# First two units of a stage alternate slab by slab, the norm's squares are added on VectorE, the first x pieces come by ScalarE's queue

## The chip, the cores and the metric

The kernel runs on one core of one Trainium2 chip. A core has TensorE (PE, matrix products into PSUM), VectorE (DVE), ScalarE (ACT), GpSimd (POOL) and SyncE (SP), each with its own in-order stream of instructions, and DMA queues that they start. The metric is the time of one execution in device microseconds (us); lower is better. Times are medians of several runs; the profile is of one further execution.

## The reference, cut to what matters

Two layers over 256 tokens of width 1024, then one last RMSNorm:

```python
for l in range(2):
    h = h + 0.5 * swiglu(rms_norm(h, ffn1_norm[l]), ...)       # 1024 -> 2816 -> 1024
    h = h + hybrid_mixer(rms_norm(h, mix_norm[l]), ...)        # z = u @ w_in, four head groups, @ w_out
    h = h + cross_attention(rms_norm(h, xattn_norm[l]), rms_norm(mem, mem_norm[l]), ...)
    h = h + 0.5 * swiglu(rms_norm(h, ffn2_norm[l]), ...)
return rms_norm(h, final_norm)

def rms_norm(x, g): return x * rsqrt(mean(x * x) + eps) * g
```

All is float32. Each stage starts with a norm of h and then a projection of all of h, so its first product needs every column of h that the stage before has just written.

## The kernel before, in words

**Layout.** `h` holds the stream transposed: 8 blocks k of 128 channels by 256 tokens. `xs` holds h times the norm's gain, each block split into a high part (ACT, L295) and the rest (DVE, L296) in the format fp32r; a product is three part products, made as one matmul of 512 columns (L361, high weights on both parts of x) and one of 256 (L362, low weights on the high part). Such a couple is called a pair below. The factor 1/rms is not in `xs`: it is applied to the products behind, so the products can start before the norm is known.

**Weights.** They come from one array in slabs of 128 by 1024 (512 KB), in the order in which `slab_plan` lists them, by SP's queue (L203) into 4 raw buffers, and each is split into high (ACT, L218) and low (DVE, L219) into 5 buffers `whl`. `W.get` hands out the next slab, splits up to 4 ahead and loads further ahead.

**Units.** A unit is 256 output columns: two slabs (i = 0 with k 0 to 3, i = 1 with k 4 to 7) of 8 pairs each, summed in one of two PSUM buffers `pj`. `proj_T` (and `pair_of` in the feed-forward stages) does a unit: slab 0, slab 1, then `join` copies the result out (ACT L369, DVE L370), which frees the PSUM buffer. After each slab `flush` runs one entry of the list `later`; that is how the norm's end is placed: `norm.rstd()` after the third slab of a stage, its use (`row_bcast`, L342) after the fourth.

**Stage starts.** `ffn` begins with units gate 0 and up 0, the mixer with qa and ka, cross attention with wq 0 and wq 1 (behind the unit V3 of the memory's projections), then `scores(0)`, which needs q of head 0. The stage before ends with `new_rows` for four pieces j of h (blocks 2j and 2j+1): split into `xs`, then `norm.add`: ACT squares the piece (L318) and POOL adds it to `acc` (L319). `rstd` adds the two halves of `acc` (POOL, L324), sums over channels on PE (L330) and takes the power on POOL (L335).

**Start of the kernel.** SP issues, in turn, a piece of x (L274), the channel constants `ch` (L276) and the slabs. **What sets the order.** The kernel is written for a framework whose planner sets each engine's order ahead of time, from its own estimates: it may put an instruction ahead of one that was written earlier if it expects that one to be held up. On the chip the order so made is fixed; an engine waits at an instruction whose inputs are late.

Of the kernel before, what the change touches and what calls it, by code (L numbers as in the profile page):

```python
# [49 lines left out]
def slab_plan():  # L50

    plan = []
    for l in range(L):
        for f in ("ffn1", "ffn2"):
            if f == "ffn2":
                plan += [("z:" + u, l, i, 1040 if "+" in u else 1024) for u in Z_ORDER for i in range(2)]
                plan += [("kv:" + u, l, i, 1024) for u in KV_EARLY for i in range(2)]
                plan += [("w_out", l, k, 1024) for k in range(KD)]
                plan += [("kv:" + u, l, i, 1024) for u in KV_LATE for i in range(2)]
                plan += [("wq:%d" % hd, l, i, 1024) for hd in range(4) for i in range(2)]  # L60
                plan += [("wo", l, k, 1024) for k in range(KD)]
            plan += [(f + ":%s:%d" % (a, g), l, i, 1024) for g in range(NG) for a in "gu" for i in range(2)]
            plan += [(f + ":dn", l, i, 1024) for i in range(NG * 2)]
    return plan

# [175 lines left out]
def trunk(ctx: ExitStack, tc: tile.TileContext, xT, memT, wall, chan, gateb, dlam, t5, poolw, c128, small, out):  # L241
# [29 lines left out]
    h = res.tile([128, KD, T], F32, name="h")  # L271
    ch = const.tile([128, N_CHAN], F32, name="ch")
    for j in range(4):
        nc.sync.dma_start(out=h[:, 2 * j:2 * j + 2, :], in_=xT[:, 512 * j:512 * j + 512].rearrange("p (a b) -> p a b", a=2))  # L274
        if j == 0:
            nc.sync.dma_start(out=ch[:], in_=chan)  # L276
        W.load()
    cc = const.tile([128, 1024], F32, name="cc")
    ident = cc[:, 0:128]
# [18 lines left out]
    class Norm:  # L298
# [12 lines left out]
        def add(self, src):  # L311
            if self.acc is None:
                self.acc = ztile("acc")[:, 0:512]
                S.activation(out=pair(self.acc), in_=src, func=AF.Square)
                self.rows = [self.acc[:, 0:256], self.acc[:, 256:512]]
                return
            sq = ztile("sq")[:, 0:512]
            S.activation(out=pair(sq), in_=src, func=AF.Square)  # L318
            G.tensor_tensor(out=self.acc, in0=self.acc, in1=sq, op=ALU.add)  # L319

        def rstd(self):
            rows = self.rows
# [12 lines left out]
            self.last = G.tensor_tensor(out=r[:], in0=m[:], in1=nhalf[:, 0:2], op=ALU.pow)  # L335
            return r
# [59 lines left out]

    def proj_T(units, l, x, evac):

        for u in units:
            p = pproj()  # L400
            for i in range(2):
                w = W.get(u, l, i, 256)
                for kk in range(4):
                    k = 4 * i + kk
                    for n in range(2):
                        mm2(p[:, n * 512:n * 512 + 512], parts(w, kk, slice(n * 128, n * 128 + 128)), x(k), k == 0, k == KD - 1)
                flush()
            evac(u, join(p))

    def proj_M(u, l, x, width):  # L410

# [52 lines left out]

    def ffn(l, name, norm, c_next, extra=()):
        fs, rbs = [], []
        def pair_of(u):

            p = pproj()
            for i in range(2):  # L470
                w = W.get(u, l, i, 256)
                for kk in range(4):
                    k = 4 * i + kk
                    for n in range(2):
                        mm2(p[:, n * 512:n * 512 + 512], parts(w, kk, slice(n * 128, n * 128 + 128)), xk(k), k == 0, k == KD - 1)
                flush()
            return join(p)

        for g in range(NG):
            gate = pair_of(name + ":g:%d" % g)  # L480

            def act(g=g, gate=gate):
                if g == 0:
                    rbs[0] = row_bcast(rbs[0])
                V.tensor_tensor(out=pair(gate[:, 0:512]), in0=pair(gate[:, 0:512]), in1=twice(rbs[0]), op=ALU.mult)  # L485
                S.activation(out=gate[:, 0:512], in_=gate[:, 0:512], func=AF.Silu)  # L486
                if g == 0:
                    rb05 = sm.tile([128, T], F32, name="rb05", tag="rb05", bufs=1)
                    S.activation(out=rb05[:], in_=rbs[0][:], func=AF.Copy, scale=0.5)
                    rbs.append(rb05)  # L490

            if g == 0:
                later.append(lambda: rbs.append(norm.rstd()))
                later.append(act)
            else:
                act()
            up = pair_of(name + ":u:%d" % g)
# [5 lines left out]
            fs.append(f)  # L503
            for e in dict(extra).get(g, ()):
                e()
        nxt = Norm(quick=c_next is None)
# [181 lines left out]
    def mixer(l, norm, c_next):  # L688
# [42 lines left out]

        def emit(u):

            if u in ("qa", "ka", "pb"):
                w = 15 if u == "pb" else 3
                t = ztile(u)
                tv = t[:, 0:2 * (T + w)].rearrange("p (a b) -> p a b", a=2)
                G.memset(tv[:, :, 0:w], 0.0)

                def ev(_, p):  # L740
                    def go():
                        V.tensor_tensor(out=tv[:, :, w:w + T], in0=pair(p[:, 0:512]), in1=twice(rstd()[1]), op=ALU.mult)
                    if u == "qa":
                        later.append(lambda: R.append(norm.rstd()))
                        later.append(go)
                    else:
                        go()
                proj_T(["z:" + u], l, xk, ev)
                z[u] = tv
# [363 lines left out]
    def cross(l, norm, kv, c_next):  # L1113
# [5 lines left out]

        def wq(hd):  # L1120

            q = big.tile([128, 1024], F32R, name="xq", tag="m", bufs=4)
            proj_T(["wq:%d" % hd], l, xk, lambda _, p: halves(p, q))
            st["q", hd] = q
            if hd == 0:
                def scale():
                    r = norm.rstd()
                    r16 = sm.tile([128, 2], F32, name="r16", tag="r16")
                    V.tensor_scalar(out=r16[:], in0=r[:], scalar1=1.0 / 16, scalar2=None, op0=ALU.mult)
                    R.append(r16)  # L1130
                later.append(scale)

        def scores(hd):
            qt, kt = st["q", hd], kv["K%d" % hd]
# [37 lines left out]
            halves(p, os_[hd])  # L1172

        wq(0)
        wq(1)
        scores(0)
        wq(2)
        scores(1)
# [43 lines left out]
```

## Time and profile before

| | us |
|---|---|
| median of 3 runs | 1213.91 (1213.82 to 1214.43) |
| the profiled execution, its own time | 1216.12 |
| its span from first to last instruction | 1214.3 |
| PE busy | 1192.7 |
| DVE busy | 864.0 |
| ACT busy | 691.2 |
| POOL busy | 109.6 |

The profile gives for each engine the instructions in order of time, what ended the idle time before one, and, for stretches, the clock that was granted to PE (1.00 is its full 2.4 GHz, 0.50 is 1.2 GHz). "issue" means that nothing in the profile explains the time.

### The profile page before, as it was taken

The numbers are of one execution on the slowest core, as the hardware profiler recorded it, in microseconds if no ns is written. First come the engines' busy times: TensorE is split into PE (matmuls) and PEld (weight loads), VectorE is DVE, ScalarE is ACT, GpSimd is POOL, SyncE is SP. The second block draws the span as 40 slices with busy tenths as digits, with TensorE's granted clock in tenths as the row PEclk, the third lists the DMA queues.
The fourth block names the chain that finished last, engine by engine and source line by source line (L and its number), as shares of the span: only waits on it lengthen the run. The fifth ranks groups of instructions, "written<-read, shape, count | busy, mean of one in ns | idle before, by whom it ended". The sixth has DMA issues, their size and how long they took to land.

```text
span 1214.3 us, 18603 instructions
## 1 busy us (share of the span) xinstructions
PE 1192.7 (98%) x7199; PEld 1050.2 (86%) x7199; DVE 864.0 (71%) x1214; ACT 691.2 (57%) x1038; POOL 109.6 (9%) x107
## 2 busy tenths in 40 slices
PE   8999999999999999999999999999999999999996
PEld 6788888988899988888888888898889998888886
DVE  5887667869667677775677776786785867777653
ACT  6766555556556555554555555555664655655552
POOL 4130001104010100000010000011220202000000
PEclk9999999999999999999999999999999999999998
DMA  8866765554445355656556567645535534555650
GB/s 267 281 203 193 225 194 174 162 185 151 144 140 191 105 188 183 197 181 199 189 172 196 184 194 225 190 161 170 183 128 163 172 131 139 185 194 183 197 178 35
DMA packets 63032, 216.48 MB, mean 178 GB/s; under 512 B 7712, under 2 KB 8112, under 8 KB 62944
## 3 DMA queue, kind: packets, MB, share of 16 engines
q1 hardware_dynamic: 61632, 212.11, 54.6%
q0 software_dynamic: 1024, 2.80, 0.8%
q8 instruction: 56, 0.92, 0.3%
q10 hardware_dynamic: 288, 0.39, 0.1%
q14 instruction: 32, 0.26, 0.1%
HBM read 210.01 MB, written 2.11 MB: 175 GB/s over the span
## 4 chain that ended last, share of the span: by engine, by line
PE 89%; DVE 6%; issue 2%; ACT 1%; DMA 1%; POOL 0%; SPq 0%; POOLq 0%; DVEq 0%; ACTq 0%
PE pj L361 49%; PE pj L362 25%; PE pj L355 2%; PE pj L356 2%; DVE whl L219 2%; PE pj L357 2%; PE pj L423 2%; DVE xs L296 1%; ACT whl L218 1%; DMA selt<-in_c_dram 1%; PE pq L357 0%; PE pq L356 0%; PE pq L355 0%; PE pq L956 0%; DMA raw<-in_wall_dram 0%
## 5 line engine op out<-in xcount | busy, mean ns | idle before, releaser
L361 PE MATMUL pj<-xs,whl 128*128 128x512 f32 x1760 | 620.9, 396 | 8.6 <-DVE xs L296 6.4
L219 DVE TENSOR_TENSOR whl<-raw,whl 128x1024 fp32r<-128x1024 f32 (+1 forms) x391 | 483.4, 1239 | 165.6 <-ACT whl L218 160.8
L218 ACT CAST whl<-raw 128x1024 fp32r<-128x1024 f32 (+1 forms) x391 | 406.0, 1042 | 177.1 <-PE pj L362 98.3
L362 PE MATMUL pj<-xs,whl 128*128 128x256 f32 x1760 | 494.6, 281 | 0.1
L361 PEld LDWEIGHTS pj<-xs,whl 128*128 128x128 f32 x1760 | 332.7, 189 | 84.6 <-DVE xs L296 9.1
L362 PEld LDWEIGHTS pj<-xs,whl 128*128 128x128 f32 x1760 | 334.9, 190 | 1.8 <-issue 0.9
L361 PE MATMUL pj<-fs,whl 128*128 128x512 f32 x704 | 244.6, 392 | 0.1
L369 ACT COPY jn<-pj 128x512 f32<-128x512 f32 x147 | 85.6, 582 | 226.6 <-PE pj L362 222.7
L370 DVE TENSOR_TENSOR jn<-pj,jn 128x512 f32<-128x512 f32 x147 | 100.9, 686 | 137.9 <-ACT jn L369 137.8
L362 PE MATMUL pj<-fs,whl 128*128 128x256 f32 x704 | 197.0, 280 | 0.0
L361 PEld LDWEIGHTS pj<-fs,whl 128*128 128x128 f32 x704 | 132.1, 188 | 29.2 <-DVE jn L370 0.2
L362 PEld LDWEIGHTS pj<-fs,whl 128*128 128x128 f32 x704 | 133.0, 189 | 0.0
L319 POOL TENSOR_TENSOR acc<-acc,sq 128x512 f32<-128x512 f32 x29 | 43.3, 1494 | 844.5 <-ACT sq L318 843.9
L296 DVE SCALAR_TENSOR_TENSOR xs<-h,ch,xs 128x256 fp32r<-128x256 f32 x64 | 42.2, 703 | 6.0 <-ACT xs L295 6.0
L361 PE MATMUL pj<-whl,ms 128*128 128x512 f32 x128 | 45.9, 400 | 0.0
L361 PE MATMUL pj<-ms,whl 128*128 128x512 f32 x128 | 45.7, 397 | 0.0
L501 ACT CAST fs<-jn 128x512 fp32r<-128x512 f32 x44 | 27.4, 622 | 24.1 <-DVE jn L498 24.1
L486 ACT ACTIVATE jn<-jn 128x512 f32<-128x512 f32 x44 | 27.8, 632 | 21.9 <-DVE jn L485 21.9
L295 ACT ACTIVATE xs<-h,ch 128x256 fp32r<-128x256 f32 x64 | 29.2, 501 | 13.2 <-DVE h L569 8.5
L355 PE MATMUL pj<-ys,whl 128*128 128x256 f32 x128 | 36.1, 282 | 0.3 <-DVE h L569 0.2
L362 PE MATMUL pj<-ms,whl 128*128 128x256 f32 x128 | 36.4, 284 | 0.0
L355 PE MATMUL pj<-os,whl 128*128 128x256 f32 x128 | 35.9, 283 | 0.4 <-DVE h L569 0.4
(263 smaller groups left out, 1305.0 us busy)
## 6 DMA issues: line engine op xcount, KB each, us to landing
raw<-in_wall_dram SPq DMA_DIRECT2D x377, 512.0 KB, 3.7
raw<-in_wall_dram SPq DMA_DIRECT2D x8, 520.0 KB, 3.7
mem<-memd SPq DMA_DIRECT2D x8, 256.0 KB, 5.1
raw<-in_wall_dram SPq DMA_DIRECT2D x6, 256.0 KB, 5.5
h<-in_xT_dram SPq DMA_DIRECT2D x4, 256.0 KB, 5.6
mem<-in_memT_dram SPq DMA_DIRECT2D x4, 256.0 KB, 6.3
br<-drow POOLq DMA_DIRECT2D x4, 256.0 KB, 6.6
memd<-mem POOLq DMA_DIRECT2D x4, 256.0 KB, 4.8
```

What stands on the lines that cost most here:

```text
L218: self.nc.scalar.copy(out=hi[:, a:a + m], in_=r[:, a:a + m])
L219: self.last = self.nc.vector.tensor_tensor(out=lo[:, a:a + m], in0=r[:, a:a + m], in1=hi[:, a:a + m].bitcast(F32), op=ALU.subtract)
L295: S.activation(out=hi, in_=src, func=AF.Copy, scale=gcol(c, k))
L296: V.scalar_tensor_tensor(out=lo, in0=src, scalar=gcol(c, k), in1=hi.bitcast(F32), op0=ALU.mult, op1=ALU.subtract)
L319: G.tensor_tensor(out=self.acc, in0=self.acc, in1=sq, op=ALU.add)
L355: PE.matmul(o, w(0), x[:, 0, :], start=first, stop=False, skip_group_check=True)
L361: PE.matmul(o.rearrange("p (s t) -> p s t", s=2), w(0), x, start=first, stop=False, skip_group_check=True)
L362: PE.matmul(o[:, 0:256], w(1), x[:, 0, :], start=False, stop=last, skip_group_check=True)
L369: S.copy(out=tv, in_=v[:, :, 1, :])
L370: V.tensor_tensor(out=tv, in0=v[:, :, 0, :], in1=tv, op=ALU.add)
L486: S.activation(out=gate[:, 0:512], in_=gate[:, 0:512], func=AF.Silu)
L501: S.copy(out=part(f, 0), in_=pair(up[:, 0:512]))
```

## The change

Three edits. (1) `proj_T` takes several units and goes slab by slab: slab 0 of each unit, then slab 1 of each, each unit joined after its slab 1. It is called with two units at the start of each feed-forward stage (gate 0, up 0), of the mixer (qa, ka) and of cross attention (wq 0, wq 1); the slab plan follows. `rstd` stays after the third slab; what uses it in the feed-forward stages and in the mixer moves from after the fourth slab to after the fifth. (2) The adds of L319 and L324 go from POOL to DVE. (3) At the kernel's start `ch` and the pieces 1 to 3 of x are issued from ACT's queue, piece 0 and the slabs from SP's.

```diff
@@ slab_plan
-  plan += [("z:" + u, l, i, 1040 if "+" in u else 1024) for u in Z_ORDER for i in range(2)]
+  plan += [("z:" + u, l, i, 1024) for i in range(2) for u in Z_ORDER[:2]]
+  plan += [("z:" + u, l, i, 1040 if "+" in u else 1024) for u in Z_ORDER[2:] for i in range(2)]
...
-  plan += [("wq:%d" % hd, l, i, 1024) for hd in range(4) for i in range(2)]
+  plan += [("wq:%d" % hd, l, i, 1024) for i in range(2) for hd in range(2)]
+  plan += [("wq:%d" % hd, l, i, 1024) for hd in range(2, 4) for i in range(2)]
...
-  plan += [(f + ":%s:%d" % (a, g), l, i, 1024) for g in range(NG) for a in "gu" for i in range(2)]
+  plan += [(f + ":%s:0" % a, l, i, 1024) for i in range(2) for a in "gu"]
+  plan += [(f + ":%s:%d" % (a, g), l, i, 1024) for g in range(1, NG) for a in "gu" for i in range(2)]
@@ trunk
     for j in range(4):
-        nc.sync.dma_start(out=h[:, 2 * j:2 * j + 2, :], in_=xT[...])
+        q = nc.scalar if j else nc.sync
         if j == 0:
-            nc.sync.dma_start(out=ch[:], in_=chan)
+            nc.scalar.dma_start(out=ch[:], in_=chan)
+        q.dma_start(out=h[:, 2 * j:2 * j + 2, :], in_=xT[...])
         W.load()
@@ Norm.add, Norm.rstd
-  G.tensor_tensor(out=self.acc, in0=self.acc, in1=sq, op=ALU.add)
+  V.tensor_tensor(out=self.acc, in0=self.acc, in1=sq, op=ALU.add)
...
-  G.tensor_tensor(out=rows[0], in0=rows[0], in1=rows[1], op=ALU.add)
+  V.tensor_tensor(out=rows[0], in0=rows[0], in1=rows[1], op=ALU.add)
@@ proj_T
-        for u in units:
-            p = pproj()
-            for i in range(2):
+        ps_ = [pproj() for _ in units]
+        for i in range(2):
+            for u, p in zip(units, ps_):
                 w = W.get(u, l, i, 256)
...
                 flush()
-            evac(u, join(p))
+                if i == 1:
+                    evac(u, join(p))
@@ ffn
+  if g == 0:
+      later.extend([lambda: None] * 2)
+      later.append(lambda: rbs.append(norm.rstd()))
+      proj_T(names, l, xk, got.__setitem__)
+      later.append(lambda got=got, names=names: finish(0, *(got[u] for u in names)))
+  else:
+      for u in names:
+          proj_T([u], l, xk, got.__setitem__)
+      finish(g, *(got[u] for u in names))
@@ mixer: emit("qa") does qa and ka in one proj_T, emit("ka") returns
+  later.extend([lambda: None] * 2)
+  later.append(lambda: R.append(norm.rstd()))
+  proj_T(list(tvs), l, xk, got.__setitem__)
+  later.append(go)
@@ cross: wq(0) does heads 0 and 1, the call wq(1) is gone
+  later.extend([lambda: None] * 2)
+  later.append(scale)
+  proj_T(["wq:%d" % i for i in hds], l, xk, lambda u, p: halves(p, st["q", int(u[3:])]))
```

## Rows read from the trace of the kernel before

**Rows 1.** The page, part 1: busy us (share of the span) xinstructions of each engine.
```profile
PE 1192.7 (98%) x7199; PEld 1050.2 (86%) x7199; DVE 864.0 (71%) x1214; ACT 691.2 (57%) x1038; POOL 109.6 (9%) x107
```
**Rows 2.** Waits of PE: line, waited for; us in total, times, longest.
```profile
PE pj L361 <- DVE xs L296: 6.4, 7, 1.9
```
**Rows 3.** PE in order of time, feed-forward start of layer 1: start, us, what.
```profile
1013.28 0.39 PE L361 MATMUL pj<-xs,whl 128*128 128x512 f32 x1
...
1017.10 0.39 PE L361 MATMUL pj<-xs,whl 128*128 128x512 f32 x1
1019.49 0.51 PE L361 MATMUL pj<-xs,whl 128*128 128x512 f32 x1 [1.88 <-DVE xs L296]
...
1025.50 0.50 PE L330 MATMUL pq<-ones,acc 128*128 128x1 f32 x4
...
1028.72 0.60 PE L342 MATMUL pq<-cc,r_tok 128*128 128x128 f32 x4
```
**Rows 4.** Stretch: us, PE, PEld, DVE, ACT, POOL busy, granted clock, DMA share, GB/s.
```profile
1021.00:1022.00 1.00, 1.00 (x5) 0.90 (x4) 1.00 (x2) 0.04 (x1) 0.00 (x0) 0.50 0.01 4
```
**Rows 5.** DVE in order of time, the same start.
```profile
1012.65 1.67 DVE L296 SCALAR_TENSOR_TENSOR xs<-h,ch,xs 128x256 fp32r<-128x256 f32 x4
...
1015.69 2.33 DVE L219 TENSOR_TENSOR whl<-raw,whl 128x1024 fp32r<-128x1024 f32 x1 [0.78 <-ACT whl L218]
1017.94 2.36 DVE L296 SCALAR_TENSOR_TENSOR xs<-h,ch,xs 128x256 fp32r<-128x256 f32 x2
```
**Rows 6.** POOL in order of time, the same start.
```profile
1017.13 2.02 POOL L319 TENSOR_TENSOR acc<-acc,sq 128x512 f32<-128x512 f32 x1 [0.19 <-ACT sq L318]
```
**Rows 7.** The page, part 5, POOL's adds: busy, mean ns, idle before.
```profile
L319 POOL TENSOR_TENSOR acc<-acc,sq 128x512 f32<-128x512 f32 x29 | 43.3, 1494 | 844.5 <-ACT sq L318 843.9
```
**Rows 8.** PE in order of time, from feed-forward 2 into the next layer.
```profile
608.19 0.40 PE L361 MATMUL pj<-xs,whl 128*128 128x512 f32 x1
...
615.40 0.50 PE L361 MATMUL pj<-xs,whl 128*128 128x512 f32 x1 [0.49 <-DVE xs L296]
...
620.58 0.61 PE L342 MATMUL pq<-cc,r_tok 128*128 128x128 f32 x4
```
**Rows 9.** DVE in order of time, the same start.
```profile
611.48 0.69 DVE L540 TENSOR_TENSOR h<-h,jn 128x512 f32<-128x512 f32 x1
612.25 1.22 DVE L219 TENSOR_TENSOR whl<-raw,whl 128x1024 fp32r<-128x1024 f32 x1
613.40 1.94 DVE L296 SCALAR_TENSOR_TENSOR xs<-h,ch,xs 128x256 fp32r<-128x256 f32 x2
```
**Rows 10.** PE in order of time, the kernel's start.
```profile
6.29 0.79 PE L361 MATMUL pj<-xs,whl 128*128 128x512 f32 x1 [0.94 <-ACT whl L218]
...
9.95 0.52 PE L361 MATMUL pj<-xs,whl 128*128 128x512 f32 x1
...
22.26 0.60 PE L342 MATMUL pq<-cc,r_tok 128*128 128x128 f32 x4
```
**Rows 11.** The kernel's start: an issue on SP, ACT's first work.
```profile
1.18 0.42 SPq L276 DMA_DIRECT2D ch<-in_chan_dram  x1
...
3.89 0.63 ACT L314 ACTIVATE acc<-h 128x512 f32<-128x512 f32 x1 [1.87 <-DMA h<-in_xT_dram]
```
**Rows 12.** Stretch of the kernel's start, columns as in rows 4.
```profile
4.00:5.00 1.00, 1.00 (x4) 0.15 (x2) 0.00 (x0) 0.58 (x2) 0.00 (x0) 1.00 0.96 342
```
**Rows 13.** DVE, then PE, in order of time behind the kernel's start.
```profile
29.52 0.16 DVE L630 CAST sel<-selt 64x4 fp32r<-64x4 f32 x1 [5.52 <-DMA selt<-in_c_dram]
...
35.22 0.50 PE L361 MATMUL pj<-xs,whl 128*128 128x512 f32 x1 [1.26 <-DVE jn L370]
```
**Rows 14.** ACT, DVE, PE in order of time, cross attention's start in layer 0.
```profile
360.96 0.59 ACT L369 COPY jn<-pj 128x512 f32<-128x512 f32 x1 [0.19 <-PE pj L362]
...
364.44 0.68 DVE L370 TENSOR_TENSOR jn<-pj,jn 128x512 f32<-128x512 f32 x1
...
372.32 0.28 PE L355 MATMUL pq<-K,xq 128*128 128x256 f32 x1
```

More of the change, by code (lines that the diff above doesn't have):

```diff
@@ L273, in trunk @@
     for j in range(4):
-        nc.sync.dma_start(out=h[:, 2 * j:2 * j + 2, :], in_=xT[:, 512 * j:512 * j + 512].rearrange("p (a b) -> p a b", a=2))
+        q = nc.scalar if j else nc.sync
         if j == 0:
-            nc.sync.dma_start(out=ch[:], in_=chan)
+            nc.scalar.dma_start(out=ch[:], in_=chan)
+        q.dma_start(out=h[:, 2 * j:2 * j + 2, :], in_=xT[:, 512 * j:512 * j + 512].rearrange("p (a b) -> p a b", a=2))
         W.load()
@@ L466, in ffn, with finish @@
         fs, rbs = [], []
[L467 to L490, printed above, removed]
-            if g == 0:
[L493 to L497, printed above, removed]
+        def finish(g, gate, up):
+            if g == 0:
+                rbs[0] = row_bcast(rbs[0])
+            V.tensor_tensor(out=pair(gate[:, 0:512]), in0=pair(gate[:, 0:512]), in1=twice(rbs[0]), op=ALU.mult)
+            S.activation(out=gate[:, 0:512], in_=gate[:, 0:512], func=AF.Silu)
+            if g == 0:
+                rb05 = sm.tile([128, T], F32, name="rb05", tag="rb05", bufs=1)
+                S.activation(out=rb05[:], in_=rbs[0][:], func=AF.Copy, scale=0.5)
+                rbs.append(rb05)
             V.tensor_tensor(out=up[:, 0:512], in0=gate[:, 0:512], in1=up[:, 0:512], op=ALU.mult)
@@ L503, in ffn @@
             fs.append(f)
+        for g in range(NG):
+            got = {}
+            names = [name + ":%s:%d" % (a, g) for a in "gu"]
+            if g == 0:
+                later.extend([lambda: None] * 2)
[6 more added lines that the diff above has]
+                finish(g, *(got[u] for u in names))
             for e in dict(extra).get(g, ()):
@@ L732, in emit, with go @@
         def emit(u):
-            if u in ("qa", "ka", "pb"):
+            if u == "ka":
+                return
+            if u in ("qa", "pb"):
                 w = 15 if u == "pb" else 3
[L736 to L749, printed above, removed]
+                tvs = {}
+                for v in ("qa", "ka") if u == "qa" else ("pb",):
+                    t = ztile(v)
+                    tvs["z:" + v] = z[v] = t[:, 0:2 * (T + w)].rearrange("p (a b) -> p a b", a=2)
+                    G.memset(z[v][:, :, 0:w], 0.0)
+                got = {}
+                def go():
+                    for n_, p in got.items():
+                        V.tensor_tensor(out=tvs[n_][:, :, w:w + T], in0=pair(p[:, 0:512]), in1=twice(rstd()[1]), op=ALU.mult)
+                if u == "qa":
+                    later.extend([lambda: None] * 2)
+                    later.append(lambda: R.append(norm.rstd()))
+                proj_T(list(tvs), l, xk, got.__setitem__)
+                if u == "qa":
+                    later.append(go)
+                else:
+                    go()
             elif u in ("qd", "kd", "qc", "kc"):
@@ L1120, in wq @@
         def wq(hd):
-            q = big.tile([128, 1024], F32R, name="xq", tag="m", bufs=4)
-            proj_T(["wq:%d" % hd], l, xk, lambda _, p: halves(p, q))
-            st["q", hd] = q
+            hds = (0, 1) if hd == 0 else (hd,)
+            for i in hds:
+                st["q", i] = big.tile([128, 1024], F32R, name="xq", tag="m", bufs=4)
             if hd == 0:
@@ L1174, in cross @@
         wq(0)
-        wq(1)
         scores(0)
```

## The prediction

> **What bounds the kernel now.** I read the busy times first. PE is busy for 1192.7 of 1214.3 us, every other engine for 71% or less [rows 1]. So the matmuls set the time, and a change that removes no matmul can only win what PE loses: the 21.6 us in which it stands, and stretches in which it runs at less than full clock. Next I read the list of PE's waits, to see where it stands. One entry carries most: the first-unit matmuls wait 6.4 us, in 7 places, for the split of x on DVE, L296 [rows 2]. In order of time the seven lie at stage starts. Two are the starts of feed-forward 2 behind cross attention, 1.88 us in layer 1 [rows 3] and 1.89 at the same place in layer 0. Three are the starts behind a feed-forward stage, 0.49 us here [rows 8] and the same within 0.01 us at the other two. The last two lie at the kernel's start, 1.1 us together. At all other stage starts PE waits 0.2 us or less for x.
>
> A wait is not the whole loss, so I measured each start against PE's own pace. Twelve pairs of L361 and L362 start at 1013.28 and the twelfth at 1017.10, so a pair takes 3.82 / 11 = 0.347 us [rows 3]. From the first pair of a stage to the broadcast of the norm (L342) lie 32 pairs and the four small matmuls of L330, 0.50 us: 32 x 0.347 + 0.50 = 11.6 us at full pace.
> - Feed-forward 2 in layer 1: 1028.72 - 1013.28 = 15.44 us, so 3.8 are lost [rows 3]. The wait is 1.88 of them. The rest is the clock: behind the wait the granted clock is 0.50 [rows 4], 1.2 instead of 2.4 GHz; before it PE had worked without a gap. Two such starts: 7.7 us.
> - Behind a feed-forward stage: 620.58 - 608.19 = 12.39, so 0.8 are lost [rows 8]. No half clock follows. Three such starts: 2.4 us.
> - The kernel's start: 22.26 - 6.29 = 15.97. The first five pairs, at half pace, take 9.95 - 6.29 = 3.66 instead of 1.74 us; those 1.9 no edit touches. 15.97 - 11.6 - 1.9 = 2.5 us are left [rows 10].
>
> So 12.6 us lie at six stage starts, and the change is aimed at them.
>
> **Why x is late.** A DVE split of a 512 KB slab takes 1.22 us when it runs alone [rows 9]. At the feed-forward start the same instruction takes 2.33, and the last two L296 take 2.36 [rows 5], where four took 1.67 just before, so 0.83 for two. While they are slow, POOL is adding squares: its L319 takes 2.02 there [rows 6], against a mean of 1.49 [rows 7]. Behind the feed-forward stages L296 takes 1.94 for two as well [rows 9]. So in these stretches a POOL add and a DVE operation on two inputs hold each other up, by about 1.1 us for each DVE operation.
>
> **Part 1, slab by slab.** It adds no matmul. Twelve pairs run before the wait at the feed-forward start [rows 3], which is k = 0 to 5 of unit one. With slab 0 of unit two ahead of slab 1 of unit one, 20 pairs run before k = 6 is wanted: 1013.28 + 20 x 0.347 = 1020.2, where PE went on at 1019.49 in the old order, even with the slow splits. So this part alone removes the wait, and with it the half clock: +3.8 us at each of two starts. At the three starts behind a feed-forward stage it brings little: from 608.19 to the wait, which begins 0.49 us before 615.40, PE issued about 19 pairs [rows 8]. That is more than the 14 of k = 0 to 6, so the planner had already put pairs of unit two ahead. Three slabs are split before a stage begins (five `whl` buffers, two still held by the stage before), and the first three slabs in the new plan are the ones wanted, so no weight is late. The uses of the norm move one slab (2.8 us) back; the conv of the mixer and the first feed-forward product are wanted far later, so I cost that at nothing.
>
> What it adds are three earlier deadlines. Unit three wants the PSUM buffer of unit one a slab after unit one ends, not two. Unit two wants its buffer 2.8 us into the stage. And `scores(0)` wants q of head 0 one slab after that unit, not after a whole unit.
> - Cross attention, unit two: wq 1 takes the buffer of V3. V3's copy starts on ACT at 360.96, but its DVE half ends only at 364.44 + 0.68 = 365.1 [rows 14], behind slowed splits. wq 1 would start at 360.96 + 2.78 = 363.7: up to 1.4 us of waiting, if DVE is no faster than before; none if it is freed of its slow stretches (1.1 for a slab split, 1.5 for the two L296).
> - Cross attention, `scores(0)`: the chain is copy 0.59, add 0.68 [rows 14], then a cast and a subtraction of the same size: 2.5 us, plus up to a slab split on the way (1.22 on DVE). It has one slab and L330, 2.78 + 0.50 = 3.3 us: a stall of 0 to 0.5, and 1.2 more with a second split.
> - I take 1.0 us for each of the two cross starts (0 to 2.6): -2.0. Queued behind these joins on DVE and ACT are the next slab splits; PE holds three ahead, so they cover it.
> - At the other starts unit one's join has 1.3 us of work in 2.78 + 0.50 us, so nothing is taken.
>
> **Part 2, squares on DVE.** POOL loses 29 adds, 43.3 us [rows 7], and nine adds of half the size. DVE gains 29 x 0.69 us, by a DVE add of this shape [rows 9], and nine of at most 0.69: 20 to 26 us on an engine with 350 us to spare [rows 1]. It gets back about 1.1 us for each of its operations that met an add, two or three at a stage start, so its sum should stay about where it is (bounds: 26 more, or as many less as POOL's adds lasted). At the feed-forward start, two new adds run (1.4 us) ahead of the slab split, then split 1.2 and the two L296 0.8: x of k = 6 is there at about 1018.0 where it was 1019.4. Where the starts lose 0.8 us, the two L296 end 1.1 us earlier than now (1.94 to 0.83) and PE lacked 0.49: +0.8 us each, +2.4 for three; with the adds put ahead of them it could be half.
>
> **Part 3, x by ACT's queue.** SP loses four issues of 0.42 us, ACT gets them: 1.7 us, in front of ACT's first operation, before which it stood 1.87 us waiting for x [rows 11]. So ACT pays nothing, and slabs are asked for up to 1.7 us earlier. But by 4 to 5 us the DMA engines are 0.96 busy at 342 GB/s [rows 12]: what arrives earlier pushes something else back. A 256 KB piece of x ahead of the first half slab is 0.75 us, and the first matmul waits for that half slab's split [rows 10]. I take the whole 0.75 off the start's 2.5: +1.7 (-0.7 to +2.5). The Trainium skill ("Trainium Kernel Development and Optimization", Key Constraints) speaks against this part: DMAs from the SP, ACT and POOL queues share the same 16 DMA engines and interleave, and several issuers save only the issue time. By that rule the start gives 1.7; if the pieces came free of charge it would give 2.5, and the total would be 0.75 us lower.
>
> **Behind the start.** At 24 to 29.5 us DVE stands 5.5 us at a cast that waits for a small DMA which POOL issues behind the first norm's power; PE loses 1.26 of it at 35.22 [rows 13]. The norm comes some 2 us earlier, so the DMA should too, but the planner may put the cast elsewhere among the joins: from -1.5 to +1.26, I take +0.4.
>
> **Sum.** 7.7 + 2.4 + 1.7 + 0.4 - 2.0 = 10.2 us. The profiled execution took 1216.12 us for a span of 1214.3, and is 2.2 above the median; so 1205.9 against itself, and 1213.9 - 10.2 = 1203.7 for a median. With every term at its good end 7.7 + 2.4 + 2.5 + 1.3 = 13.9: 1200.0. With every term at its bad end 6.0 + 1.0 - 0.7 - 1.5 - 5.2 = -0.4: 1214.3.
>
> **The rivals.**
> - Order without effect, 1205.6. The planner, which already mixed units at three starts, might lay the pairs much as before, and only part 2 works. Then x of k = 6 at 1018.0 meets a want at 1017.45: 0.6 us lost, probably without half clock: 2 x 3.2 + 2.4 + 1.5 - 2.0 = 8.3. For it: rows 8. Against it: at the two costly starts the planner had kept the written order [rows 3].
> - New waits eat half, 1209. The two cross starts at their full 2.6 us, the cast behind the kernel's start at -1.5, and the three small starts at half: 7.7 + 1.2 + 1.7 - 1.5 - 5.2 = 3.9, and with a gain at the kernel's start of 2.5 some 5. For it: DVE is the busiest engine behind PE at each start, and V3's join ended 4.1 us after its copy began.
> - Slower, 1216. The same join delay at every stage start: if a unit's join takes the 4.1 us that V3's took, unit three waits 4.1 + 0.2 - 2.78 = 1.5 us at each of eight starts, 12 us, or twice that where half clock follows. It decides from 10.2 / 8 = 1.3 us a start on. Against it: at the feed-forward starts the joins now begin at once and DVE stands waiting for them.
>
> **How the numbers follow.** Forecast 0.60 (1203.7; its own range 1200 to 1207), order without effect 0.14, new waits 0.21, slower 0.05. Predicted is the forecast's 1203.7. The range takes in the bounds on the good side, 1199.5, and the new waits at 1209 with a little more, 1210.5. This kernel's measurement tells 0.2%, 2.4 us, from no change, so faster means below 1211.5. Of the new waits' 0.21, 0.08 lie above that: faster 0.60 + 0.14 + 0.13 = 0.87, same 0.08, slower 0.05.
>
> **What the profile after would show.** Right: no wait for L296 above 0.2 us at the feed-forward starts, the granted clock at 1.00 behind them, first pair to 40th pair (the new place of L342) at 0.347 us each, slab splits on DVE at 1.22 us throughout, POOL below 60 us, DVE within 25 us of 864. Wrong: waits of L361 or L355 for `jn` or `xq` at the cross starts, a first matmul later than 7.1 us, a DVE stand of over 5 us at the cast with more than 1.3 us of PE lost behind it, or slabs that are late at L218.

## The result, and the profile after

The changed kernel takes 1205.53 us (median of 4 runs, 1205.52 to 1205.56), the kernel before on the same chip 1214.17. The ratio is 0.9926, 95% interval 0.9909 to 0.9944: faster by some 8.6 us. Predicted were 1203.7 us, 1.8 us too few. Its profiled execution took 1205.53 us for a span of 1203.8, so from trace to trace 10.5 us of span are gone (1214.3 - 1203.8).

Busy times first, columns as in [rows 1], then the three largest waits of TensorE, columns as in [rows 2]:

```profile
PE 1186.3 (99%) x7199; PEld 1047.2 (87%) x7199; DVE 862.2 (72%) x1252; ACT 692.9 (58%) x1038; POOL 54.3 (5%) x69
```
```profile
PE pj L365 <- DVE xs L300: 2.5, 1, 2.5
PE pj L365 <- ACT sgo L800: 2.1, 2, 1.1
PE pq L334 <- ACT sq L312: 1.9, 1, 1.9
```

L361, L296 and L219 of before are L365, L300 and L222 here. The seven waits for x are one, at the kernel's start. New is the second line, two waits of 1.05 us for `sgo`. DVE took over 38 adds and is 1.8 us less busy than before. The adds and the splits, grouped by line (busy us, mean ns | idle before), show why:

```profile
L323 DVE TENSOR_TENSOR acc<-acc,sq 128x512 f32<-128x512 f32 x29 | 19.9, 687 | 0.1
L328 DVE TENSOR_TENSOR acc<-acc 128x256 f32<-128x256 f32 x9 | 3.8, 420 | 0.1
L300 DVE SCALAR_TENSOR_TENSOR xs<-h,ch,xs 128x256 fp32r<-128x256 f32 x64 | 28.0, 478 | 6.8 <-ACT xs L299 6.8
L222 DVE TENSOR_TENSOR whl<-raw,whl 128x1024 fp32r<-128x1024 f32 (+1 forms) x391 | 473.7, 1215 | 173.3 <-ACT whl L221 167.9
```

The adds cost 19.9 + 3.8 = 23.7 us. An `xs` split now takes 478 ns in the mean; at the starts of before it took up to 1.2 us [rows 5].

The feed-forward start of layer 1, PE in order of time, answers [rows 3]; the stretch behind the place of the old wait, columns as in [rows 4], stands under it:

```profile
1007.05 0.39 PE L365 MATMUL pj<-xs,whl 128*128 128x512 f32 x1
...
1015.38 0.50 PE L334 MATMUL pq<-ones,acc 128*128 128x1 f32 x4
...
1021.38 0.60 PE L346 MATMUL pq<-cc,r_tok 128*128 128x128 f32 x4
```
```profile
1015.00:1016.00 1.00, 1.00 (x9) 0.96 (x8) 1.00 (x2) 0.42 (x1) 0.00 (x0) 1.00 0.87 336
```

From 1007.05 to 1021.38 are 14.33 us for 40 pairs and L334: 40 x 0.347 + 0.50 = 14.38. Nothing is lost, and the granted clock is 1.00 where it was 0.50. DVE at this start (compare [rows 5]): the adds stand ahead of the slab split, and each operation has its short duration.

```profile
1008.01 0.69 DVE L323 TENSOR_TENSOR acc<-acc,sq 128x512 f32<-128x512 f32 x1
...
1009.21 0.68 DVE L323 TENSOR_TENSOR acc<-acc,sq 128x512 f32<-128x512 f32 x1
1009.81 1.22 DVE L222 TENSOR_TENSOR whl<-raw,whl 128x1024 fp32r<-128x1024 f32 x1
1010.95 0.88 DVE L300 SCALAR_TENSOR_TENSOR xs<-h,ch,xs 128x256 fp32r<-128x256 f32 x2
```

The new wait, in the mixer of layer 0: ACT, DVE and PE in order of time.

```profile
225.70 0.46 ACT L800 ACTIVATE sgo<-pj,rh 128x256 f32<-128x256 f32 x1
226.95 0.58 ACT L373 COPY jn<-pj 128x512 f32<-128x512 f32 x1 [0.79 <-PE pj L366]
227.43 0.48 ACT L800 ACTIVATE sgo<-pj,rh 128x256 f32<-128x256 f32 x1
```
```profile
214.59 0.69 DVE L744 TENSOR_TENSOR qa<-jn,rb 128x512 f32<-128x512 f32 x1
...
226.77 0.21 DVE L797 SCALAR_TENSOR_TENSOR fg<-pj,r_tok,gb 128x4 f32<-128x4 f32 x1
```
```profile
227.96 0.50 PE L365 MATMUL pj<-xs,whl 128*128 128x512 f32 x1 [1.05 <-ACT sgo L800]
```

PE wants a PSUM buffer that `fg` on DVE and the tanh `sgo` on ACT still read. `fg` is through at 226.98, behind the convolution, and ACT's order now has the copy of the unit just ended (L373) ahead of the second `sgo`. PE stands from 226.91 to 227.96. The second `sgo` takes 0.48 us: begun at 226.98, right behind `fg`, it would have ended at 227.46. So by these rows `fg` accounts for about half of the 1.05 us, and the copy ahead of `sgo` for the rest.

Where the 10.5 us lie, by PE's marks in the traces of both kernels, from first product to first product of the stages (us; the two layers as a pair):

| stretch | before | after | gain |
|---|---|---|---|
| kernel's start to first w_down product of feed-forward 1 | 139.24 | 136.62 | 2.62 |
| from there to w_out, which holds the mixer | 192.90, 192.92 | 193.23, 193.39 | -0.80 |
| w_out to wo, which holds the cross start | 59.45, 59.46 | 59.53, 59.57 | -0.19 |
| wo to w_down of feed-forward 2 | 155.53, 155.76 | 151.83, 151.80 | 7.66 |
| w_down of feed-forward 2 to that of the next feed-forward 1 | 185.00 | 184.12 | 0.88 |
| first w_down product of the last feed-forward 2 to the end | 74.02 | 73.66 | 0.36 |

### The profile page after: what moved, and what is told of

It reads as the page before. It is cut to its first block, busy times and chain, and to the rows that moved or that the text cites. A ratio compares the mean times of both kernels' runs of the same rounds, so it can differ in the third digit from the quotient of the medians.

```text
span 1203.8 us, 18570 instructions
## 1 busy us (share of the span) xinstructions
PE 1186.3 (99%) x7199; PEld 1047.2 (87%) x7199; DVE 862.2 (72%) x1252; ACT 692.9 (58%) x1038; POOL 54.3 (5%) x69
## 4 chain that ended last, share of the span: by engine, by line
PE 94%; DVE 4%; ACT 1%; DMA 0%; issue 0%; POOLq 0%; DVEq 0%; ACTq 0%
PE pj L365 52%; PE pj L366 27%; PE pj L359 2%; PE pj L360 2%; PE pj L361 2%; PE pj L428 2%; DVE whl L222 1%; PE pq L361 0%; PE pq L360 0%; PE pq L359 0%; PE pq L960 0%; PE pq L889 0%; PE pq L942 0%; ACT whl L221 0%; PE pq L1036 0%; PE pq L941 0%
## 5 line engine op out<-in xcount | busy, mean ns | idle before, releaser
L365 PE MATMUL pj<-xs,whl 128*128 128x512 f32 x1760 | 616.3, 394 | 4.6 <-DVE xs L300 2.5
L222 DVE TENSOR_TENSOR whl<-raw,whl 128x1024 fp32r<-128x1024 f32 (+1 forms) x391 | 473.7, 1215 | 173.3 <-ACT whl L221 167.9
L365 PEld LDWEIGHTS pj<-xs,whl 128*128 128x128 f32 x1760 | 331.0, 188 | 77.2 <-ACT whl L221 3.0
L365 PE MATMUL pj<-fs,whl 128*128 128x512 f32 x704 | 244.6, 392 | 0.1
L373 ACT COPY jn<-pj 128x512 f32<-128x512 f32 x147 | 85.7, 583 | 208.0 <-PE pj L366 206.1
L365 PEld LDWEIGHTS pj<-fs,whl 128*128 128x128 f32 x704 | 132.1, 188 | 29.1 <-DVE jn L374 0.2
L365 PE MATMUL pj<-ms,whl 128*128 128x512 f32 x128 | 46.4, 402 | 0.0
L365 PE MATMUL pj<-whl,ms 128*128 128x512 f32 x128 | 45.9, 400 | 0.0
L339 POOL TENSOR_TENSOR r_tok<-ms,nhalf 128x2 f32<-128x2 f32 x10 | 7.9, 787 | 801.9 <-DVE ms L338 801.9
L359 PE MATMUL pj<-os,whl 128*128 128x256 f32 x128 | 35.9, 283 | 0.4 <-DVE h L566 0.4
L360 PE MATMUL pj<-os,whl 128*128 128x256 f32 x128 | 35.9, 281 | 0.2
```

Source lines behind the costliest of these rows:

```text
L222: self.last = self.nc.vector.tensor_tensor(out=lo[:, a:a + m], in0=r[:, a:a + m], in1=hi[:, a:a + m].bitcast(F32), op=ALU.subtract)
L359: PE.matmul(o, w(0), x[:, 0, :], start=first, stop=False, skip_group_check=True)
L360: PE.matmul(o, w(0), x[:, 1, :], start=False, stop=False, skip_group_check=True)
L365: PE.matmul(o.rearrange("p (s t) -> p s t", s=2), w(0), x, start=first, stop=False, skip_group_check=True)
L373: S.copy(out=tv, in_=v[:, :, 1, :])
```

## The experiments

Unless said otherwise a run's time is the median of its runs, with the ratio to the kernel before on the same chip.

**The kernel before, once more.** No edit. The question was whether the half clock behind the two long waits belongs to the kernel or to one execution.

> The kernel before, unchanged, profiled a second time, because its first profiled execution took 2.2 us more than its median. If the half clock behind the two feed-forward 2 starts is not the same in every execution, this profile shows it at one of the two starts or at none and its span is about 1212, some 2 us less than in the first profile; if it is the same in every execution, both starts lose 3.8 us again and the span is 1214. Untraced median 1213.9 either way.

It took 1213.12 us (10 runs, 1210.63 to 1215.58). Its profiled execution, 1215.58 us, had both half clocks again, with a span of 1213.8 us, as the expectation's second branch had it. But the executions differ. Over the 46 of the kernel before that were run beside the kernels below, time and granted clock go together: 1210.7 to 1212.0 us in the seven with a mean granted clock of 0.998, 1213.6 to 1215.4 in the seven with 0.993, 1217.0 in the one with 0.992. Of the ten here, three had 0.998 and took 1210.6 to 1212.3 us, but the one with 0.992 took 1213.5, so the mean clock doesn't settle the time alone. The trace of before, 1216.12 us, was among the dear ones.

The trace of part 3 alone (below) shows that the wait need not bring the half clock. Its feed-forward 2 starts are those of before, with waits of 1.88 and 1.92 us, and the granted clock stays at 1.00. Layer 1, the wait and a stretch behind it (compare [rows 3] and [rows 4]):

```profile
1022.31 0.50 PE L362 MATMUL pj<-xs,whl 128*128 128x512 f32 x1 [1.92 <-DVE xs L297]
```
```profile
1024.00:1025.00 1.00, 1.00 (x8) 0.86 (x7) 1.00 (x2) 0.75 (x2) 0.00 (x0) 1.00 0.00 0
```

From the first pair to the norm's broadcast that kernel takes 13.89 and 13.94 us at these two starts, the kernel before 15.29 and 15.44. So of the 3.8 us lost at such a start about 2.3 are there without half clock, and about 1.5 come with it.

**Part 1 alone.** `slab_plan`, `proj_T`, `ffn`, mixer and cross attention as in the change; the adds stay on POOL, x on SP's queue.

```diff
-  V.tensor_tensor(out=self.acc, in0=self.acc, in1=sq, op=ALU.add)
+  G.tensor_tensor(out=self.acc, in0=self.acc, in1=sq, op=ALU.add)
-        q = nc.scalar if j else nc.sync
+        q = nc.sync
```

> Part 1 alone: the two units of a stage start alternate slab by slab, the squares are added on POOL, x comes by SP's queue. By the theory that the order alone cures the two feed-forward 2 starts: 3.8 us at each (5.5 to 7.7 for both), nothing at the three small starts, up to 1.3 at the cast behind the start, and the mixer's new wait for sgo costs 1.05 in each layer: 1207 to 1210. By the rival that POOL's adds hold DVE up and the order matters little: the wait for L296 stays at 1 us or more at those starts and the time is 1212 or more.

1210.84 us, ratio 0.9983 (0.9974 to 0.9992), just above the theory's 1207 to 1210. The feed-forward 2 stretch falls to 151.89 us, so the alternating alone does remove wait and half clock there. Much of it is paid back at the cross starts, where w_out to wo rises from 59.45 to 61.31 us, and in the mixers (the same two waits for `sgo`, 1.05 us each). In this trace the kernel's start is longer too, 140.56 us against 139.24: PE waits 1.61 us for POOL's last add, and the granted clock is 0.50 behind that. The cross start in this kernel, PE, DVE and POOL:

```profile
366.87 0.50 PE L364 MATMUL pj<-xs,whl 128*128 128x512 f32 x1 [1.47 <-DVE jn L373]
```
```profile
359.28 2.34 DVE L222 TENSOR_TENSOR whl<-raw,whl 128x1024 fp32r<-128x1024 f32 x1 [0.78 <-ACT whl L221]
361.54 2.40 DVE L299 SCALAR_TENSOR_TENSOR xs<-h,ch,xs 128x256 fp32r<-128x256 f32 x2
363.86 2.35 DVE L222 TENSOR_TENSOR whl<-raw,whl 128x1024 fp32r<-128x1024 f32 x2
366.14 0.68 DVE L373 TENSOR_TENSOR jn<-pj,jn 128x512 f32<-128x512 f32 x1
```
```profile
360.72 2.05 POOL L322 TENSOR_TENSOR acc<-acc,sq 128x512 f32<-128x512 f32 x1 [0.18 <-ACT sq L321]
```

While POOL adds, one slab split takes 2.34 us; as soon as it has stopped, two take 2.35. The join of V3 (L373) stands behind them, and the wait is the 1.4 us that the prediction had as its bound.

**Part 2 alone.**

```diff
-  G.tensor_tensor(out=self.acc, in0=self.acc, in1=sq, op=ALU.add)
+  V.tensor_tensor(out=self.acc, in0=self.acc, in1=sq, op=ALU.add)
-  G.tensor_tensor(out=rows[0], in0=rows[0], in1=rows[1], op=ALU.add)
+  V.tensor_tensor(out=rows[0], in0=rows[0], in1=rows[1], op=ALU.add)
```

> Part 2 alone: the squares are added on DVE, the order of the units and the queues are those of before. By the theory that POOL's adds slow DVE by about 1.1 us for each operation they meet, x of k = 6 comes 1.4 us earlier at the feed-forward 2 starts, the wait falls from 1.9 to 0.6 us or less and the half clock does not come: 2 x 3.0 there, 0.8 at each small start, nothing lost in the mixer: 1204.5 to 1207. By the rival that only the order cures the large starts: they keep a wait of 1 us or more, and the time is 1211 or more.

1202.83 us, ratio 0.9921 (0.9908 to 0.9935), below the range of either theory: two lines give all that the whole change gives. Feed-forward 2 takes 151.96 us, the stretch behind it 184.28, the mixer 192.15, the cross stretch is unchanged at 59.45. DVE at the feed-forward start of layer 1, where the first pair starts at 1006.00:

```profile
1006.99 0.69 DVE L319 TENSOR_TENSOR acc<-acc,sq 128x512 f32<-128x512 f32 x1
...
1008.20 0.69 DVE L319 TENSOR_TENSOR acc<-acc,sq 128x512 f32<-128x512 f32 x1
1008.80 1.22 DVE L219 TENSOR_TENSOR whl<-raw,whl 128x1024 fp32r<-128x1024 f32 x1
1009.93 0.87 DVE L296 SCALAR_TENSOR_TENSOR xs<-h,ch,xs 128x256 fp32r<-128x256 f32 x2
```

In the old order of pairs, k = 6 is wanted at 1006.00 + 12 x 0.347 = 1010.16 and PE does not stand for it: the three waits for x that this kernel has, 3.1 us together, all lie at its start. So parts 1 and 2 are two cures of one wait, and their gains don't add: 151.89 with the first, 151.96 with the second, 151.83 with both.

**Part 3 alone.**

```diff
-        nc.sync.dma_start(out=h[:, 2 * j:2 * j + 2, :], in_=xT[...])
+        q = nc.scalar if j else nc.sync
         if j == 0:
-            nc.sync.dma_start(out=ch[:], in_=chan)
+            nc.scalar.dma_start(out=ch[:], in_=chan)
+        q.dma_start(out=h[:, 2 * j:2 * j + 2, :], in_=xT[...])
```

> Part 3 alone: ch and x pieces 1 to 3 from ACT's queue. By the trace of the changed kernel the first matmul comes at 7.46 instead of 6.29 us, since ACT's table load of 1.28 us now stands behind the wait for x. Then the later x pieces come earlier and PE waits less for them at the start. Theory: a loss of up to 1.2 us, 1213.9 to 1215.1. Rival: the earlier x pieces win back more than that, 1213 or less.

1216.34 us, ratio 1.0028 (1.0013 to 1.0044): slower, and by more than the theory's 1.2 us. The first w_down product comes at 143.51 us where it came at 139.24. PE's first x product waits until 7.50, and the norm's sum then waits for POOL, whose adds of one start follow each other at 1.7 us each:

```profile
21.81 1.01 PE L331 MATMUL pq<-ones,acc 128*128 128x1 f32 x4 [3.96 <-POOL acc L325]
```
```profile
15.06 5.03 POOL L320 TENSOR_TENSOR acc<-acc,sq 128x512 f32<-128x512 f32 x3 [13.32 <-ACT sq L319]
20.16 1.59 POOL L325 TENSOR_TENSOR acc<-acc 128x256 f32<-128x256 f32 x1
```

Behind that wait the granted clock is 0.50 (24 to 25 us). The two feed-forward 2 stretches are 1.4 and 1.7 us shorter than before, because the clock stayed at 1.00 there in this execution.

**Parts 1 and 2, x on SP's queue.** The change without its third part, so the diff just above taken back.

> The changed kernel with part 3 undone: parts 1 and 2, all of x and ch from SP's queue. Theory: ACT's queue costs the 1.2 us by which the first matmul came later (7.46 against 6.29), so first matmul at 6.0 to 6.6 and 1204.0 to 1204.6. Rival: the earlier x pieces are worth as much as the late first matmul, 1205.3 or more.

1205.33 us (1204.0 to 1207.0), ratio 0.9930 (0.9918 to 0.9943), so 2.5 us behind part 2 alone and level with the whole change. The first x product comes at 5.70 us, earlier than the theory had it; the time is the rival's. The mixer stretch is 193.28 us against 192.15 with part 2 alone: this is where adding part 1 costs.

**Part 2, and part 1 in the feed-forward stages alone.** Mixer and cross attention go unit by unit as before.

```diff
   plan += [("z:" + u, l, i, 1040 if "+" in u else 1024) for u in Z_ORDER for i in range(2)]
...
   plan += [("wq:%d" % hd, l, i, 1024) for hd in range(4) for i in range(2)]
...
+  plan += [(f + ":%s:0" % a, l, i, 1024) for i in range(2) for a in "gu"]
+  plan += [(f + ":%s:%d" % (a, g), l, i, 1024) for g in range(1, NG) for a in "gu" for i in range(2)]
```

> Part 2, and part 1 in the feed-forward stages alone: mixer and cross attention as before. Theory: at the feed-forward starts part 1 and part 2 cure the same wait, so the second adds nothing there, but at the kernel's start, where part 2 alone still waits 2.2 us for x, the alternation gives up to 2.2; the mixer's wait for sgo does not come: 1200.5 to 1202.5. Rival: the alternation costs something at the feed-forward starts too: 1203 or more.

1202.08 us (1201.3 to 1203.0), ratio 0.9901 (0.9886 to 0.9916), as the theory had it and below parts 1 and 2 (1205.33); the interval overlaps that of part 2 alone. Mixer 192.15, cross 59.44, feed-forward 2 151.84 us. Against part 2 alone the traces differ at the kernel's start (first w_down product at 136.25 against 137.87), but that isn't shown to be the order's doing: behind the first pair PE stands 2.0 us in this trace, now for weights (1.45) and for POOL (0.59), and 2.4 in the other, and the granted clock at 12 to 13 us is 1.00 here and 0.50 there.

**The convolution behind the gates.** Parts 1 and 2, with an entry of the mixer's order moved, to bring `fg` and `sgo` ahead of the convolution on DVE.

```diff
-qa  ka  va+ia conv  oa+fa gates  qd
+qa  ka  va+ia  oa+fa gates conv  qd
```

> Parts 1 and 2, and the mixer's conv written behind the gates instead of ahead of them. Theory: in the changed kernel PE waits 1.05 us in each layer for sgo's tanh to free a PSUM buffer, because the small DVE operations on the same PSUM result stand behind conv on DVE, and conv came a slab later. With conv behind them the wait is gone: 2.1 us less than parts 1 and 2 alone, some 1202.3. Rival: the wait has another cause (ACT's own order) and stays, within 0.5 us of parts 1 and 2.

1204.62 us, ratio 0.9925 (0.9913 to 0.9938), against 1205.33: no more than a hint of a gain, and neither expectation came. The waits for `sgo` are gone; a later wait has grown in their place, and ACT changes tables once more (1.28 us, L828). PE's waits in this kernel, columns as above, against 0.5 us for `e` in the changed kernel:

```profile
PE pq L959 <- DVE e L977: 3.0, 2, 1.5
```

ACT in this kernel also shows that the second `sgo` comes behind the second `fg`, as the reading of the wait above has it:

```profile
222.77 0.47 ACT L799 ACTIVATE sgo<-pj,rh 128x256 f32<-128x256 f32 x1 [0.29 <-DVE fg L796]
```

So moving the convolution back only moves the wait: the whole chain behind qa and ka is late.

**qa and ka multiplied behind the fourth slab.** Parts 1 and 2; the use of the norm in the mixer is back where it was in slabs.

```diff
-                if u == "qa":
-                    later.append(go)
-                else:
-                    go()
+                go()
```

> Parts 1 and 2 of the change, but in the mixer the products qa and ka are multiplied right behind the fourth slab, not behind the fifth. Theory (the later qa/ka push the convolution and the gate on VectorE, so the second half of sgo on ScalarE comes about 1 us late for TensorE in each layer): the wait for sgo, 2 times 1.05 us, goes, and the time is about 2.1 us below that of parts 1 and 2 (1205.33 us), some 1203.2 us. Rival (the alternating of the first two units costs it by itself, through PSUM buffers and joins): the wait stays or another comes in its place, and the time is within 0.5 us of 1205.3.

1201.85 us (1201.6 to 1203.1), ratio 0.9897 (0.9882 to 0.9911). No wait for `sgo` is left, and the mixers take 192.01 and 192.08 us. The alternating itself costs nothing there. Of the 5.0 us between the two spans (1205.2 and 1200.2) 2.6 lie in the mixers; 1.9 lie ahead of the first w_down product, where the edit changes nothing, so I took that for the start's own scatter. The clock is a part of it. A matmul of 512 columns still takes 0.63 us at 12.66 in the trace of parts 1 and 2, and 0.39 at 11.99 here:

```profile
12.66 0.63 PE L364 MATMUL pj<-xs,whl 128*128 128x512 f32 x1
```
```profile
11.99 0.39 PE L364 MATMUL pj<-xs,whl 128*128 128x512 f32 x1
```

**The same edit in the changed kernel,** to tell the mixers' share from the scatter of the start.

> The changed kernel, all three parts, with qa and ka in the mixer multiplied right behind the fourth slab, not behind the fifth. Theory (the uses of the norm that went back one slab in the mixer cost TensorE 1.05 us of standing and some 0.2 us more at each of two places, as between parts 1 and 2 with and without it: 193.28 and 192.01 us from the first w_down product to the first w_out product): no wait for sgo, each mixer 1.2 to 1.3 us shorter than the changed kernel's 193.23, and 1202.6 to 1203.4 us where the changed kernel took 1205.53. Rival (the gain between those two kernels lay at the kernel's start, which was 1.9 us shorter in the trace, and was chance): the wait goes, something else takes its place, and the time is above 1204.5 us.

1203.28 us, ratio 0.9908 (0.9892 to 0.9925), against 1205.53. The start is the changed kernel's (136.84 against 136.62), the mixers take 192.01 and 192.03 against 193.23 and 193.39. So the norm's late use costs 2.6 us in the traces and 2.25 between the medians. DVE and ACT in the mixer of this kernel:

```profile
210.89 0.68 DVE L744 TENSOR_TENSOR qa<-jn,rb 128x512 f32<-128x512 f32 x1
```
```profile
225.40 0.47 ACT L797 ACTIVATE sgo<-pj,rh 128x256 f32<-128x256 f32 x1
...
227.29 0.57 ACT L373 COPY jn<-pj 128x512 f32<-128x512 f32 x1
```

The product qa starts 4.7 us behind the mixer's norm sum on PE (L334 at 206.24), as it did before, where it was 8.6 in the changed kernel (214.59, L334 at 206.03). The second `sgo` is ahead of the copy again and done when PE comes for its buffer.

**An early table for ACT.** The changed kernel with a tiny activation at the head of ACT's stream. In the changed kernel ACT begins with DMA issues, and the load of its table waits for x with the first activation:

```profile
0.74 0.41 ACTq L279 DMA_DIRECT2D ch<-in_chan_dram  x1
1.18 1.42 ACTq L280 DMA_DIRECT2D h<-in_xT_dram  x3
5.00 1.28 ACT L299 ACT_TABLE_LOAD   x1 [5.00 <-DMA h<-in_xT_dram]
```
```diff
+    early = const.tile([128, 1], F32, name="early")
+    G.memset(early[:], 1.0)
+    S.activation(out=early[:], in_=early[:], func=AF.Copy, scale=1.0)
```

> The changed kernel, all three parts, with one 128x1 activation on ACT ahead of the first wait for x, so that the 1.28 us load of ACT's table runs while x is on its way. Theory: the late first matmul came from the table load behind the wait for x: first matmul at 6.2 to 6.5, 1204.2 to 1204.7. Rival: it came from piece 0 of x landing at 5.0 instead of 3.9 us, among pieces 1 to 3: first matmul at 7.0 or later, 1205 or more.

1205.29 us, ratio 0.9929 (0.9916 to 0.9941): nothing gained. The table loads at 2.63 and the first x product starts at 6.83 instead of 7.46, so the late table was about half of the 1.2 us. But the matmuls of 512 columns behind it run at half pace, 0.63 us each, for longer: the last such begins at 12.20 us in this trace, at 10.81 in the changed kernel's. That isn't shown to come from the edit, for the warm-up ahead of them already differs: its last matmul takes 0.63 us here and 0.38 there.

**Part 3 on the best order.** The kernel with part 1 in the feed-forward stages alone, and x by ACT's queue (the diff of part 3).

> Part 2, part 1 in the feed-forward stages alone, and part 3. Theory (behind part 2 the third part is worth nothing, as it was on top of parts 1 and 2: 1205.33 against 1205.53 us): 1202.1 us within 0.7, as without part 3 (1202.08). Rival (the first activation's late table, 1.28 us behind the wait for x, is paid in full): 1203 us or more.

1203.64 us, where the rival wanted 1203 or more, but the ratio is 0.9909 (0.9892 to 0.9925), which overlaps that of the kernel without part 3, and the kernel before took 1.6 us more on this chip than on that one's. In the traces the first w_down product is 1.3 us later than without part 3 (137.54 against 136.25), and the rest is the same. With qa and ka early it is 0.7 us later (136.84 against 136.10), and 1203.28 against 1201.85 us. With qa and ka late it is the other way, 136.62 with part 3 and 137.97 without, so one pair of traces decides nothing here. By the medians part 3 gains nothing, and may cost about 1 us.

**Part 3, early table, longer warm-up.** To the kernel just above come the early activation and

```diff
-    for _ in range(9):
+    for _ in range(13):
```

> Part 2, part 1 in the feed-forward stages alone, part 3, a tiny activation ahead of ScalarE's DMA starts so that its table is loaded early, and 13 warm-up matmuls in place of 9. Theory (the start is held by the first x and by the half clock that follows TensorE's standing between the warm-up and the first x): the first pair at about 6.8 us, no stretch of matmuls at half clock behind it, 1200 to 1201.3 us. Rival (the clock falls all the same, or something behind the start sets the end of the first stage): 1202 us or more.

1203.13 us, ratio 0.9905 (0.9890 to 0.9920). No matmul runs at half pace behind the first x product, which is at 6.98, as the theory wanted; the time is the rival's all the same. That the longer warm-up did it isn't shown: the kernel with neither part 3 nor the longer warm-up has no half pace there either. PE in order of time here, and then in that kernel (1202.08 us):

```profile
6.98 0.50 PE L366 MATMUL pj<-xs,whl 128*128 128x512 f32 x1 [1.28 <-ACT whl L219]
...
9.52 0.73 PE L366 MATMUL pj<-xs,whl 128*128 128x512 f32 x2 [0.37 <-ACT whl L219]
...
20.48 0.58 PE L335 MATMUL pq<-ones,acc 128*128 128x1 f32 x4 [0.94 <-ACT jn L374]
```
```profile
6.10 0.47 PE L362 MATMUL pj<-xs,whl 128*128 128x512 f32 x1 [1.33 <-DVE xs L297]
...
9.59 0.73 PE L362 MATMUL pj<-xs,whl 128*128 128x512 f32 x2 [1.45 <-ACT whl L219]
```

PE goes on at 9.5 to 9.6 in both, though its first product came 0.9 us apart: it wants ACT's split of weights. ACT begins that at 8.85 and 8.92, in the first kernel when the weights land (0.32 us of waiting for DMA), in the second behind a wait of 1.46 us for x. So in these two traces PE's first product isn't what bounds the start; what ACT waits for from DMA is.

## Why the prediction came out as it did

**Feed-forward 2, right for this trace.** 2 x 3.8 = 7.7 was forecast, 3.70 + 3.96 = 7.66 measured. But 3.1 of that are half clock, which an execution may or may not have: with the same waits and without it the two stretches take 154.09 and 154.11 us, so there the gain would be 4.6. The text took the half clock for a consequence of the wait. It gave the gain to part 1, which does it; but part 2 does it too. The text had part 2 come 0.6 us short of that (its first rival); the rows of part 2 alone show x just in time.

**Starts behind a feed-forward stage, right in size.** 2.4 forecast; 0.88 measured at the one that stands alone. At the two in front of a mixer the gain shows with qa and ka early: 192.90 to 192.01 and 192.92 to 192.03, 0.89 each. That makes 2.7.

**Uses of the norm one slab back, wrong.** This is the step of the text that failed: "The conv of the mixer and the first feed-forward product are wanted far later, so I cost that at nothing." In the feed-forward stages that holds. In the mixer the convolution is early work on DVE, and `fg` is queued behind it; behind `fg` comes the second `sgo` on ACT, and only then is the PSUM buffer free. The product qa came 3.9 us later, not 2.8. Cost: 2.6 us. The text had asked who waits for the result, and not who is queued behind it on DVE and ACT.

**Cross starts, wrong the other way.** -2.0 forecast, -0.2 measured. The mechanism is real, as part 1 alone shows: w_out to wo is longer by 1.9 us there. With POOL quiet it is gone. The text had named both ends, "none if it is freed of its slow stretches", and with part 2 in the same change that end was the nearer. The join of V3, which ended 4.1 us behind its copy's start before [rows 14], ends 1.3 us behind it now, and no product waits for it:

```profile
358.66 0.59 ACT L373 COPY jn<-pj 128x512 f32<-128x512 f32 x1 [0.19 <-PE pj L366]
```
```profile
359.31 0.68 DVE L374 TENSOR_TENSOR jn<-pj,jn 128x512 f32<-128x512 f32 x1
```

**Start and cast, right in sum alone.** 1.7 + 0.4 forecast, 2.62 measured. The cast behind the start no longer waits, so the whole 1.26 us [rows 13] came back:

```profile
28.90 0.15 DVE L627 CAST sel<-selt 64x4 fp32r<-64x4 f32 x1
```

The remaining 1.4 us can't be credited to part 3, by the medians with and without it (1205.53 and 1205.33 us). From the first pair to the 40th the start now loses little but its half clock (16.36 us against 14.38 at full pace, with the clock at 0.50 for 3.4), but the first pair comes at 7.46, not 6.29 [rows 10], past the 7.1 that the text had set as a sign of error: "ACT pays nothing" forgot the table load, which waits for x with the first activation. The Trainium skill ("Trainium Kernel Development and Optimization", Key Constraints) says that issuing DMAs from several engines saves only the issue time. The runs agree in that no order of the work became faster by part 3 (1216.34 us alone, against 1213.16); they don't tell the shared DMA engines from the late table.

**Part 2, right.** POOL 54.3 us against "below 60", DVE 1.8 us below 864.0, splits at 1.22 us. What each side pays when both run is in the rows of part 1 alone: 2.34 us for a split, 2.05 for an add. The Trainium skill ("SBUF — State Buffer", SBUF: two separate sides) says that an operation of DVE with two inputs in SBUF and a GpSimd operation that reads SBUF exclude each other for a whole instruction. The trace agrees that both suffer; it does not tell exclusion from sharing.

**The sum and the median.** Terms measured: 7.7 + 2.7 + 2.6 - 0.2 - 2.6 + 0.4 (the end, not forecast) = 10.6 by the rounded terms, 10.5 by the spans, against 10.2 forecast. Two errors, 2.6 us lost in the mixers and 1.8 not lost at the cross starts, nearly cancelled: that the sum came out so close is luck. Against the profiled execution the text gave 1205.9, and 1205.53 it was. The miss of 1.8 us is in the last line, "1213.9 - 10.2 = 1203.7 for a median". That trace was 2.2 us above its median, and the two half clocks, 3.1 us, are a part of what differs between executions. The change takes away what made that execution dear, so 1203.7 counts some of the same microseconds twice. That the two half clocks make up the whole 2.2 us is argued from clock and time, and not shown stretch by stretch in the unprofiled runs.

**Left open.** What decides whether half clock follows a wait. Why the changed kernel repeats within 0.04 us where its neighbours scatter by 1 to 3 us. And which of the best two orders is the better: 1202.08 and 1201.85 us come from different sets of runs, with overlapping intervals.

## What to carry to other kernels

When an instruction is moved back, follow what is queued behind it on its engine down to the next buffer that it frees; "its result is wanted later" is only half the question. When two parts of a change cure the same wait, credit it once, and try the cheaper one alone: here two lines that take adds off POOL gave the whole gain. And if the profiled execution is dearer than the median by the very thing that the change removes, subtract from that execution, not from the median.

## What the chip showed unexpectedly

- The same kernel gets a different share of full clock from execution to execution: before, 0.992 to 0.998 in the mean, with 1217.0 to 1210.7 us. The same wait of 1.9 us of PE was followed by 3.4 us at 0.50 in both traces of the kernel before, and by none in the trace of part 3 alone.
- At the kernel's start the time that PE stood doesn't decide alone whether half clock follows. Behind 1.33 us there was none (part 2, and part 1 in feed-forward alone: matmuls of 0.39 us), behind 0.72 us there was (parts 1 and 2 with qa and ka early: 0.63 us). In the first the same nine warm-up matmuls had already come up to full pace, 3.45 us in all, in the second they had not, 4.02 us:

```profile
1.32 3.45 PE L445 MATMUL pj<-warm 128*128 128x512 bf16 x9 [1.32 <-POOL nhalf L287]
...
6.94 0.39 PE L362 MATMUL pj<-xs,whl 128*128 128x512 f32 x1
```
```profile
1.32 4.02 PE L447 MATMUL pj<-warm 128*128 128x512 bf16 x9 [1.32 <-POOL nhalf L289]
...
7.07 0.63 PE L364 MATMUL pj<-xs,whl 128*128 128x512 f32 x1
```

- Moving DMA issues to the head of ACT's stream put its table load, 1.28 us, from 0.74 us behind the first x, at 5.00.
